# One transformer layer on one core: attention's weight folds with gate blocks between them, the merge kept in SBUF, and longer loads in the planner's model

## The chip, the core and the metric

The kernel runs on one core of a Trainium2 chip. The metric is the device time of one execution in microseconds, lower is better. A figure for the kernel is the median of several runs.

## What is computed

One layer for 1024 frames of width 1024, all in float32. A normed input h is projected to the inputs of two recurrent branches and to two merge gates; the branches' outputs are merged, and cross attention to 256 memory tokens and an MLP follow.

```python
h = rmsnorm(x, norm_mix_g)
proj = h @ w_in                      # ..., gate_a, gate_b
y_a = o_a @ w_branch_gdn             # gated DeltaNet branch
y_b = o_b @ w_branch_gla             # gated linear attention branch
merged = sigmoid(gate_a) * y_a + sigmoid(gate_b) * y_b
x = x + merged @ w_out
q = rmsnorm(x) @ wq;  k = rmsnorm(mem) @ wk;  v = rmsnorm(mem) @ wv     # 4 heads
x = x + softmax(q k^T / 16) v @ wo
x = x + relu(rmsnorm(x) @ w1)**2 @ w2
out = rmsnorm(x)
```

## The kernel before, in words

**Precision and engines.** A product in float32 is made of three matmuls in a reduced float format (`mm3`, L529): the high part of both factors, high times low, low times high (L534, L536, L538). `split` (L572) makes the two parts of an operand: ACT copies the high part (L574), DVE or POOL subtracts it for the low part (L575). Weights come by DMA from the SP queue into a tile `raw` (L503, four buffers), are split into `wop` and `wlo` tiles, and are used by PE (TensorE). A result leaves PSUM by an operation of ACT or DVE (VectorE); there are four PSUM buffers named `pd` and four named `ps`.

**Stages.** In order of the program: phase 0 (norms, and all of cross attention that depends on memory alone), four gate blocks, the linear attention branch (GLA), the DeltaNet branch, the merge, the output projection, attention, the MLP. Most large products use a seven-product scheme for 2x2 blocks (`wino`, p = 0..6).

**Phase 0** (`phase0`, L678). `project("wk", u)` and `project("wv", u)` make keys and values of the memory tokens, a quarter (u) at a time, from two 512 KB loads each: K0..K3, V0..V3, 48 matmuls of 256 columns each. Their results go to tile `kv` (L724, L725), which has one buffer, for keys first, for values later. `fold_q(h)` multiplies the query weights of a head with its keys, so that attention needs no queries (Q0..Q3, 48 matmuls of 256 columns each); DVE evicts to `gst` (L740, three buffers), and a DMA from the ACT queue stores it to `Gd`. `fold_o(h)` does the same for the output weights and values (O0..O3, 24 matmuls of 512 columns each); ACT evicts (L754), stored to `Ud`. The order is K0..K3, Q0..Q3, V0, O0, V1, O1, V2, O2, V3, O3. Between them `x_norm` norms each half of x: sums, a reciprocal root, eight scalings by DVE (L764) and eight splits into `hb`, which the gates and GLA read. `XO` names the blocks after which x is loaded, summed and normed.

**Gate blocks.** `push_gate` (L1438) multiplies h with 128 columns of the gate weights (48 matmuls of 512 columns), ACT takes tanh, and the result is stored to `tgd` in DRAM. Gates 0 to 3 run after phase 0; under them `t_sums` (L798) makes the sums of x that GLA's products need and splits them.

**The merge** (`phase_merge`, L1761). `yb` forms y_b for output blocks in two pairs; `yb_done` multiplies by the gate, read back from `tgd` through a ring of eight pieces in tile `A0b`, and stores the product to `m1d` in DRAM. `ya` forms y_a; `ya_done` reads gate and m1d back (two ring pieces for each block and half), multiplies and adds; the first four blocks go to `md` in DRAM and are read back by `staged` (L1549), the last four are split at once. `put` splits the merged blocks into `B0a`/`B0b` and `B1a`/`B1b`, which the output projection reads.

**What sets the order.** A planner (`Plan`, L159) first records the whole program, then lists it again: `latest` works backwards from PE's times to a due time for each operation, `forward` simulates the engines and takes the ready operation that is due first, PE in program order among those that are ready. The result is a fixed order on each engine's queue; a waiting instruction holds all those behind it. Costs are in `Op` (L74): a DMA takes its bytes at 390 bytes per ns on one ring and 2050 ns to land.

Of the kernel before, what the change touches and what calls it, by code (L numbers as in the profile page):

```python
# [18 lines left out]
P = 128  # L19
# [22 lines left out]
XO = (('K3', 'Q1', 'V0'), ('V0', 'V1', 'O2'))  # L42
# [21 lines left out]
ROUNDS, TOP, PAD, WINDOW, LOAD, HORIZON = 4, 228656, 128, 3413, 1283, 30000  # L64
# [9 lines left out]
class Op:  # L74
# [6 lines left out]
    def __init__(self, ins, flex):  # L81
# [33 lines left out]
        if ins.opcode == "DMACopy":  # L115
            self.dma, self.cost, self.own, self.lat = True, 60, 2050, 2050
            self.bytes = n * 4 * outs[0].ap[0][1]
        elif eng == "tensor":
            m = size(ins_[0])
            if ins.is_transpose:  # L120
                self.cost = m * 0.85
            elif ins_[0].dtype == F32R:
                self.cost = m * 0.4463 + (4 if m < HALF else 0)
            elif m == 64:
# [34 lines left out]
class Plan:  # L159
# [119 lines left out]
    def latest(self, deps, at, end):  # L279

        ops, n = self.ops, len(self.ops)
        last = [end] * n
        users, order = [0] * n, []
        for d in deps:
            for j in d:
                users[j] += 1
        todo = [i for i in range(n) if not users[i]]
        while todo:
            i = todo.pop()
            o = ops[i]  # L290
            s = last[i] = at[i] if o.eng == "tensor" else last[i] - o.cost
            for j in deps[i]:
                q = ops[j]
                if q.eng != "tensor":
                    last[j] = min(last[j], s - q.to(o, j in self.raw[i]) - q.bytes / 390)
                users[j] -= 1
                if not users[j]:
                    todo.append(j)
        return last

    def forward(self, deps, prio):
# [35 lines left out]
        def run(i, t):  # L337
# [18 lines left out]
            if o.dma:  # L356
                e = free["ring"] = max(e, free["ring"]) + o.bytes / 390
# [113 lines left out]
class Layer:  # L471
# [206 lines left out]
    def phase0(self, xp):  # L678
        nc, a = self.nc, self.a
        with ExitStack() as ctx:  # L680
# [1080 lines left out]
    def phase_merge(self, sp, ob):  # L1761
# [27 lines left out]

        def yb_done(u):  # L1790
            def done(i, half, x):
                nc.vector.scalar_tensor_tensor(x, get(), 1.0, x, ADD, MUL)
                self.nc.sync.dma_start(self.m1d[2 * u + i][:, hs(half)], x)
                more()
            return done
# [8 lines left out]
        x[0] = self.slot("A0a", (NB, HALF), F32)  # L1804
        srcs = []
        for us in pairs:
            for i, half in stages:
                for u in us:
                    srcs += [self.tgd[2 * u + i][:, hs(half)], self.m1d[2 * u + i][:, hs(half)]]
        get, more = fetcher(srcs)  # L1810
        for k in range(0, NB, 2):
            self.load(x[0][:, k:k + 2], a["xT"][:, k:k + 2, 0:HALF])
# [7 lines left out]
        def ya_done(u, last):  # L1820
            def done(i, half, c):
                ta, m1 = get(), get()
                nc.vector.scalar_tensor_tensor(c, ta, 1.0, c, ADD, MUL)
                nc.vector.tensor_tensor(c, m1, c, ADD)
                more()
                more()
                blk = 2 * u + i
                if not last:
                    nc.sync.dma_start(self.md[blk][:, half], c)
                elif half in mT:  # L1830
                    put(blk, half, c)
                else:
                    held.append((blk, half, c))
            return done

        def after(p):

            for half in range(2):
                if p == 2 * half + 1:
# [3 lines left out]
                    for blk in range(4):  # L1843
                        put(blk, half, self.staged(sp, self.md[blk][:, half]))
# [7 lines left out]
        x[1] = self.slot("A0b", (NB, HALF), F32)  # L1852
        for k in range(0, NB, 2):
            self.load(x[1][:, k:k + 2], a["xT"][:, k:k + 2, HALF:T])
# [365 lines left out]
    def run(self):  # L2220
# [7 lines left out]
        self.md = [dt([P, 2, HALF], f"md{b}") for b in range(4)]  # L2228
# [8 lines left out]
        self.m1d = [dt([P, T], f"m1d{k}") for k in range(NB)]  # L2237
# [5 lines left out]
        with ExitStack() as ctx:  # L2243
            self.wp = self.pool(ctx, "w1", "right")
            with ExitStack() as xctx:
# [3 lines left out]
                with ExitStack() as gctx:  # L2249
                    gp = self.pool(gctx, "gp", "right")  # L2250
                    for i in range(4):
# [3 lines left out]
                    self.until("g2")  # L2255
# [23 lines left out]
        with ExitStack():  # L2279
            self.phase_merge(sp, ob)  # L2280
            self.phase_out(sp)
            self.phase_attn(sp)
# [102 lines left out]
```

## Time and profile before

| | |
|---|---|
| median of 3 runs | 2214.92 us (2212.59 to 2218.59) |
| profiled execution | 2218.4 us |
| its span | 2216.6 us |
| mean granted clock | 0.991 |
| PE busy | 2160.5 us, 97% |
| DVE busy | 1702.1 us, 77% |
| ACT busy | 1092.8 us, 49% |
| moved by DMA | 300.20 MB |

Times inside the profile count from the start of the span. A row of windows gives, for a stretch, the busy time of each engine with the number of its instructions (x), the share of TensorE's full clock that was granted, the busy share of the 16 DMA engines and what they moved in GB/s. A row of waits names the engine and tile that waited, the one that ended the wait, and total, number and longest. A row of groups gives busy time and the mean in ns of one, then the idle time before them.

### The profile page before, as it was taken

What the parts mean: (1) busy time and instruction counts of PE and PEld (TensorE: products, weight loads), DVE (VectorE), ACT (ScalarE), POOL (GpSimd) and SP (SyncE); (2) the same over time, 40 slices, a digit from 0 to 9 for tenths busy, and PEclk for the clock granted to TensorE, in tenths of its full rate; (3) what the DMA queues carried; (4) which work ended last, traced back from release to release, by engine and by line L of the source; (5) the groups of instructions that cost most, each with busy time, mean ns of one, the idle gap of its engine ahead of it and who ended that gap; (6) DMA issues with size and microseconds to landing.
All of it is one profiled execution on the core that took longest, in us unless ns stands there. A gap on an engine that the chain in (4) does not pass through costs nothing.

```text
span 2216.6 us, 32151 instructions
## 1 busy us (share of the span) xinstructions
PE 2160.5 (97%) x11504; PEld 1835.2 (83%) x11504; DVE 1702.1 (77%) x3161; ACT 1092.8 (49%) x2215; POOL 208.2 (9%) x242
## 2 busy tenths in 40 slices
PE   8899999999999999999999999999999999999996
PEld 8788878988889888888878778998788888887876
DVE  7776997778796978969689965479989777567666
ACT  5544555354455545555544343465655555433433
POOL 0000000010220323222110000000100000000001
PEclk9999999999999999999999999999999999999998
DMA  8842122121311112112177841255354445687752
GB/s 273 273 153 73 59 101 86 57 83 49 120 38 50 65 47 74 48 35 76 40 248 256 285 175 67 77 168 184 116 184 142 152 157 182 212 265 249 239 175 84
DMA packets 147311, 300.20 MB, mean 135 GB/s; under 512 B 15688, under 2 KB 22216, under 8 KB 147152
## 3 DMA queue, kind: packets, MB, share of 16 engines
q1 hardware_dynamic: 140352, 289.75, 39.5%
q10 hardware_dynamic: 6800, 8.42, 1.1%
q8 instruction: 90, 1.47, 0.3%
q14 instruction: 69, 0.57, 0.1%
HBM read 212.35 MB, written 85.75 MB: 134 GB/s over the span
## 4 chain that ended last, share of the span: by engine, by line
PE 71%; DMA 11%; DVE 11%; ACT 2%; issue 2%; SPq 1%; POOL 0%; DVEq 0%; ACTq 0%; POOLq 0%
PE pd L538 18%; PE pd L534 18%; PE pd L536 18%; DMA raw<-in_w_dram 3%; PE ps L534 2%; PE ps L538 2%; PE ps L536 2%; DVE wop L575 2%; PE ps L606 1%; DMA e<-ad 1%; PE ps L1327 1%; DMA Gd<-gst 1%; SPq L503 1%; DMA A0b<-tgd 1%; DMA rawa<-pd 1%
## 5 line engine op out<-in xcount | busy, mean ns | idle before, releaser
L574 ACT ACTIVATE wop<-raw 128x512 fp32r<-128x512 f32 (+1 forms) x472 | 312.6, 669 | 377.1 <-PE pd L538 174.6
L575 DVE TENSOR_TENSOR wop<-raw,wop 128x512 fp32r<-128x512 f32 (+1 forms) x435 | 309.6, 713 | 79.4 <-ACT wop L574 77.4
L1185 DVE SCALAR_TENSOR_TENSOR acc<-pd,convw,acc 128x511 f32<-128x511 f32 x144 | 106.8, 742 | 15.7 <-ACT acc L1182 15.5
L538 PE MATMUL pd<-t,wop 128*128 128x512 f32 x268 | 107.9, 402 | 0.1
L534 PE MATMUL pd<-t,wop 128*128 128x512 f32 x268 | 106.0, 395 | 1.3 <-ACT wop L574 1.3
L536 PE MATMUL pd<-t,wop 128*128 128x512 f32 x268 | 105.1, 392 | 0.0
L534 PE MATMUL pd<-B1a,wop 128*128 128x512 f32 (+1 forms) x220 | 82.9, 377 | 0.3 <-ACT wop L574 0.3
L538 PE MATMUL pd<-B1a,wop 128*128 128x512 f32 (+1 forms) x220 | 82.8, 376 | 0.1
L538 PE MATMUL pd<-A1a,wop 128*128 128x512 f32 x180 | 73.5, 409 | 2.3 <-DVE wop L575 2.3
L534 PE MATMUL pd<-A1a,wop 128*128 128x512 f32 x180 | 72.4, 402 | 2.7 <-DVE u L1723 2.0
L536 PE MATMUL pd<-A1a,wop 128*128 128x512 f32 x180 | 71.7, 399 | 0.0
L574 ACT ACTIVATE whi<-raw 128x512 fp32r<-128x512 f32 x70 | 42.0, 626 | 55.3 <-PE pd L536 50.1
L536 PE MATMUL pd<-B0b,wop 128*128 128x512 f32 x172 | 67.6, 393 | 0.9 <-DVE B0b L575 0.9
L534 PE MATMUL pd<-A1b,wop 128*128 128x512 f32 x144 | 57.8, 402 | 3.3 <-DVE u L1723 3.3
L534 PEld LDWEIGHTS pd<-t,wop 128*128 128x128 f32 x268 | 50.4, 188 | 12.7 <-ACT wop L574 2.0
L538 PEld LDWEIGHTS pd<-t,wop 128*128 128x128 f32 x268 | 50.4, 188 | 12.6 <-DVE wop L575 1.0
L536 PEld LDWEIGHTS pd<-t,wop 128*128 128x128 f32 x268 | 50.4, 188 | 11.6
L538 PE MATMUL pd<-A1b,wop 128*128 128x512 f32 x144 | 57.5, 399 | 0.1
L536 PE MATMUL pd<-B1a,wop 128*128 128x512 f32 (+1 forms) x156 | 57.3, 367 | 0.0
L536 PE MATMUL pd<-A1b,wop 128*128 128x512 f32 x144 | 56.9, 395 | 0.0
L534 PE MATMUL pd<-A0a,whi 128*128 128x512 f32 x140 | 55.6, 397 | 0.8 <-ACT whi L574 0.8
L538 PE MATMUL pd<-A1a,wlo 128*128 128x512 f32 x140 | 56.3, 402 | 0.0
(603 smaller groups left out, 6996.4 us busy)
## 6 DMA issues: line engine op xcount, KB each, us to landing
raw<-in_w_dram SPq DMA_DIRECT2D x120, 256.0 KB, 3.9
raw<-in_w_gdn_dram SPq DMA_DIRECT2D x64, 256.0 KB, 2.8
raw<-in_w_dram SPq DMA_DIRECT2D x32, 512.0 KB, 4.4
e<-ad SPq DMA_DIRECT2D x63, 256.0 KB, 4.7
ad<-q SPq DMA_DIRECT2D x45, 256.0 KB, 2.6
rawa<-ad SPq DMA_DIRECT2D x42, 256.0 KB, 4.6
A0b<-tgd SPq DMA_DIRECT2D x32, 256.0 KB, 4.9
ad<-acc SPq DMA_DIRECT2D x30, 256.0 KB, 2.3
```

Source lines behind the costliest of these rows:

```text
L503: self.nc.sync.dma_start(dst, src)
L534: nc.tensor.matmul(out, lh, rh, start=first and i == 0, stop=False)
L536: nc.tensor.matmul(out, lh, rl, start=False, stop=False)
L538: nc.tensor.matmul(out, ll, rh, start=False, stop=last and i == n - 1)
L574: nc.scalar.activation(hi, raw, AF.Copy)
L575: (lo_eng or nc.gpsimd).tensor_tensor(lo, raw, hi.bitcast(F32), SUB)
L606: self.nc.tensor.transpose(pt[:, i * P:(i + 1) * P], s, self.ident)
L1185: nc.vector.scalar_tensor_tensor(x, pt[:, 0:HALF - d], tap, x, MUL, ADD)
L1327: nc.tensor.matmul(pt[0:96, i * n:(i + 1) * n], PF[:, v + i, 0:96], Z, start=True, stop=True)
```

## The change

1. Phase 0 makes all keys and values first; `kv` gets two buffers. Then the folds follow with gates 0 to 2 between them: Q0, Q1, g0, Q2, O0, g1, Q3, O1, g2, O2, O3. The new `gate` takes tanh into a tile with the tag `mraw`. Only gate 3 runs after phase 0. `XO` moves the norms of x accordingly.
2. The merge keeps its eight blocks in SBUF, four in slot `A0a` and four in a new pool `m`. The tensors `m1d` and `md` go; the ring holds gates alone. The first half of x is loaded to `A0a` only after its blocks are split.
3. The planner's model: a DMA lands after 2600 ns instead of 2050 and moves 300 bytes per ns instead of 390; an ACT instruction with a broken access pattern costs 140 ns more, a second output of one that reads SBUF 240 instead of 385; a small matmul is recognised by either side.

```diff
-XO = (('K3', 'Q1', 'V0'), ('V0', 'V1', 'O2'))
+ORDER = ('Q0', 'Q1', 'g0', 'Q2', 'O0', 'g1', 'Q3', 'O1', 'g2', 'O2', 'O3')
+XO = (('K3','V1','V3'),('V1','V3','Q1'))
...
-            self.dma, self.cost, self.own, self.lat = True, 60, 2050, 2050
+            self.dma, self.cost, self.own, self.lat = True, 60, LAND, LAND
...
-            self.cost, self.own, self.lat = d - 100 + (240 if psum(ins_[0]) else 385) * (len(outs) > 1), 130, 135
+            self.cost, self.own, self.lat = d - 100 + 240 * (len(outs) > 1) + 140 * broken, 130, 135
...
-                e = free["ring"] = max(e, free["ring"]) + o.bytes / 390
+                e = free["ring"] = max(e, free["ring"]) + o.bytes / RATE
...
-                    kv[which] = self.til(sp, [P, 2, NB, MEM], "kv", F32R, bufs=1)
+                    kv[which] = self.til(sp, [P, 2, NB, MEM], "kv", F32R, bufs=2)
...
-            for u in range(4):
-                self.push(f"K{u}", project("wk", u))
-            for h in range(XH):
-                self.push(f"Q{h}", fold_q(h))
-            for u in range(4):
-                self.push(f"V{u}", project("wv", u))
-                self.push(f"O{u}", fold_o(u))
+            tanh = {}
+            def gate(i):
+                def evict(half, pt):
+                    if i // 2 not in tanh:
+                        tanh[i // 2] = self.til(sp, [P, NB, MEM], "mraw", bufs=1).rearrange("p a b -> p (a b)")
+                    o = (2 * (i % 2) + half) * HALF
+                    t = tanh[i // 2][:, o:o + HALF]
+                    nc.scalar.activation(t, pt, AF.Tanh, scale=0.5)
+                    nc.sync.dma_start(self.tgd[i][:, half * HALF:(half + 1) * HALF], t)
+                return self.g_fm(lambda: self.wpart(a["w_gate"][i], [NB, P], nc.vector, sp), evict)
+            for which, x in (("K", "wk"), ("V", "wv")):
+                for u in range(4):
+                    self.push(f"{which}{u}", project(x, u))
+            makes = {"Q": fold_q, "O": fold_o, "g": gate}
+            for x in ORDER:
+                self.push(x, makes[x[0]](int(x[1])))
...
+        m = [self.slot("A0a", (4, T), F32), self.til(self.mp, [P, 4, T], "m")]
+        mb = lambda blk, half: m[blk // 4][:, blk % 4, hs(half)]
...
-                nc.vector.scalar_tensor_tensor(x, get(), 1.0, x, ADD, MUL)
-                self.nc.sync.dma_start(self.m1d[2 * u + i][:, hs(half)], x)
+                nc.vector.scalar_tensor_tensor(mb(2 * u + i, half), get(), 1.0, x, ADD, MUL)
...
-                ta, m1 = get(), get()
-                nc.vector.scalar_tensor_tensor(c, ta, 1.0, c, ADD, MUL)
-                nc.vector.tensor_tensor(c, m1, c, ADD)
+                blk = 2 * u + i
+                nc.vector.scalar_tensor_tensor(c, get(), 1.0, c, ADD, MUL)
                 more()
-                more()
-                blk = 2 * u + i
-                if not last:
-                    nc.sync.dma_start(self.md[blk][:, half], c)
-                elif half in mT:
+                to = c if last else mb(blk, half)
+                nc.vector.tensor_tensor(to, mb(blk, half), c, ADD)
+                if last and half in mT:
                     put(blk, half, c)
...
-                        put(blk, half, self.staged(sp, self.md[blk][:, half]))
+                        put(blk, half, mb(blk, half))
+                    if half:
+                        load_x(0)
...
-                    for i in range(4):
+                    for i in range(3, 4):
                         self.push_gate(i, lambda src: self.wpart(src, [NB, P], self.nc.vector), gp, "tg", 4)
```

The change moves instructions on every engine. Three places show it. The changed kernel's lines stand a little lower in its file (L505 there is L503 here, L1451 is L1436).

PE in phase 0, before: the last matmuls of V0 (they write `pd_901` and read the normed memory `mT`), then O0, which reads `kv`, the tile that V0's eviction fills.

```order
L538 MATMUL pd_901<-mT_206,wlo_896 128x256
L534 MATMUL pd_901<-mT_206,wop_895 128x256
L536 MATMUL pd_901<-mT_206,wop_895 128x256
L538 MATMUL pd_901<-mT_206,wlo_896 128x256
L534 MATMUL pd_966<-wop_955,kv_887 128x512
L536 MATMUL pd_966<-wlo_956,kv_887 128x512
L534 MATMUL pd_991<-wop_955,kv_887 128x512
```

PE in phase 0, now: the last matmuls of V3, then Q0, which reads `kv_195`, the keys' tile.

```order
L536 MATMUL pd_767<-mT_194,wop_761 128x256
L538 MATMUL pd_767<-mT_194,wop_761 128x256
L540 MATMUL pd_767<-mT_194,wlo_762 128x256
L536 MATMUL pd_832<-kv_195,wop_821 128x256
L538 MATMUL pd_832<-kv_195,wop_821 128x256
L540 MATMUL pd_832<-kv_195,wlo_822 128x256
```

The fold behind a projection no longer reads what that projection has just made.

The SP queue in the merge, before: ring loads for `ya` (gates `tgd` and products `m1d`, into `A0b`) with stores of finished blocks to `md` among them.

```order
L503 DMA A0b_12277<-tgd_101 128x512
L503 DMA A0b_12277<-tgd_100 128x512
L503 DMA A0b_12277<-m1d_160 128x512
L503 DMA A0b_12277<-m1d_161 128x512
L1829 DMA md_66<-acc_12481 128x512
L503 DMA A0b_12277<-tgd_102 128x512
L503 DMA A0b_12277<-m1d_162 128x512
L503 DMA A0b_12277<-tgd_103 128x512
L1829 DMA md_65<-q_12383 128x512
```

The SP queue there, now: gates alone, with weights of the DeltaNet branch's projection between them.

```order
L505 DMA A0b_12249<-tgd_97 128x512
L505 DMA A0b_12249<-tgd_96 128x512
L505 DMA A0b_12249<-tgd_98 128x512
L505 DMA A0b_12249<-tgd_96 128x512
L505 DMA A0b_12249<-tgd_99 128x512
L505 DMA A0b_12249<-tgd_98 128x512
L505 DMA A0b_12249<-tgd_97 128x512
L505 DMA raw_12471<-in_w_bgdn_dram 128x1024
L505 DMA A0b_12249<-tgd_99 128x512
```

All eight pieces of the ring are gates now, and no store stands between the loads.

The SP queue ahead of the merge, before: staged pieces of the linear attention's output (`obd`), stores of DeltaNet's (`oad`), then the first weights `w_bgla`.

```order
L503 DMA e_11364<-obd_71 128x512
L1436 DMA oad_78<-v_10733 128x512
L503 DMA e_11368<-obd_71 128x512
L1436 DMA oad_82<-v_10733 128x512
L503 DMA raw_11317<-in_w_bgla_dram 128x1024
L503 DMA raw_11318<-in_w_bgla_dram 128x1024
```

The same place now.

```order
L505 DMA e_11339<-obd_66 128x512
L1451 DMA oad_78<-v_10717 128x512
L505 DMA e_11343<-obd_67 128x512
L1460 DMA tgd_110<-acc_11440 128x512
L505 DMA raw_11301<-in_w_bgla_dram 128x1024
L505 DMA raw_11302<-in_w_bgla_dram 128x1024
```

Before, three of the four pieces of operand 2 (`obd_71`) are loaded ahead of the weights; now one of them (`obd_67`, the same operand) is.

More of the change, by code (lines that the diff above doesn't have):

```diff
@@ L123, in __init__ @@
                 self.cost = m * 0.4463 + (4 if m < HALF else 0)
-            elif m == 64:
+            elif max(m, size(ins_[1])) == 64:
                 self.cost = 80
@@ L294, in latest @@
                 if q.eng != "tensor":
-                    last[j] = min(last[j], s - q.to(o, j in self.raw[i]) - q.bytes / 390)
+                    last[j] = min(last[j], s - q.to(o, j in self.raw[i]) - q.bytes / RATE)
                 users[j] -= 1
@@ L1803, in phase_merge, with load_x @@
         x = self.xT = {}
[L1804 to L1812, printed above, removed]
+        get, more = fetcher([self.tgd[2 * u + i][:, hs(half)] for us in pairs for i, half in stages for u in us])
+        def load_x(half):
+            x[half] = self.slot(("A0a", "A0b")[half], (NB, HALF), F32)
+            for k in range(0, NB, 2):
+                self.load(x[half][:, k:k + 2], a["xT"][:, k:k + 2, hs(half)])
         def put(blk, half, c):
@@ L1851, in phase_merge @@
         self.drain()
-        x[1] = self.slot("A0b", (NB, HALF), F32)
-        for k in range(0, NB, 2):
-            self.load(x[1][:, k:k + 2], a["xT"][:, k:k + 2, HALF:T])
+        load_x(1)
     def sq_sum(self, sp):
```

16 lines of the change are left out of this document (8 added, 8 removed).

## The prediction

> **What bounds the kernel now.** I read the page first, then the windows by stage, then who waited for whom.
>
> ```profile
> PE 2160.5 (97%) x11504; PEld 1835.2 (83%) x11504; DVE 1702.1 (77%) x3161; ACT 1092.8 (49%) x2215; POOL 208.2 (9%) x242
> PEclk9999999999999999999999999999999999999998
> ```
>
> PE is the bound as a whole, but 97% hides waits, because the ends of matmuls are modelled. Counts in a window show them:
>
> ```profile
> core 0: us, PE busy (x) PEld busy (x) DVE busy (x) ACT busy (x) POOL busy (x), PEclk, DMA share, GB/s
> 28.00:42.00 14.00, 14.00 (x121) 14.00 (x120) 9.42 (x17) 5.51 (x8) 0.00 (x0) 1.00 0.73 220
> 1750.00:1800.00 50.00, 50.00 (x221) 41.11 (x220) 38.20 (x60) 26.76 (x43) 0.00 (x0) 1.00 0.42 145
> ...
> 42.00:65.00 23.00, 18.35 (x147) 17.46 (x146) 14.49 (x30) 6.36 (x6) 1.01 (x1) 1.00 0.88 282
> 65.00:125.00 60.00, 54.44 (x310) 46.82 (x309) 47.43 (x71) 39.31 (x62) 4.70 (x3) 0.94 0.74 243
> ...
> 1243.00:1298.00 55.00, 49.01 (x196) 36.45 (x195) 52.60 (x87) 19.71 (x34) 0.00 (x0) 0.96 0.82 291
> 1280.00:1303.00 23.00, 18.11 (x63) 12.98 (x62) 21.60 (x36) 9.84 (x17) 0.00 (x0) 0.85 0.51 173
> ```
>
> At full pace a matmul of 256 columns takes 14/121 = 0.116 us, one of 512 takes 50/221 = 0.226 us. So 42 to 65 us (Q folds) lost 23 - 147 x 0.116 = 5.9 us, and 1243 to 1298 us (end of the merge) lost 55 - 196 x 0.226 = 10.7 us. The granted clock fell in two places: 0.94 over 60 us is 3.6 us lost, 0.85 over 23 us is 3.4 us. Elsewhere nearly every window has its 221. The change aims at these two places, so the waits there are what can be won.
>
> **Keys' and values' projections first, gates between the folds.** Who waited up to 125 us: PE first, then DVE, then the stores of a fold's results (size and median landing).
>
> ```profile
> PE pd L534 <- ACT mT L689: 5.4, 1, 5.4
> PE pd L534 <- ACT kv L724: 5.4, 3, 3.3
> PE pd L534 <- DVE gst L740: 4.6, 4, 1.5
> ...
> DVE gst L740 <- DMA Gd<-gst: 12.4, 7, 3.1
> ...
> Gd<-gst ACTq DMA_DIRECT2D x16, 256.0 KB, 5.5
> ```
>
> - The wait for kv (5.4 us): each O fold stood right behind the projection whose result it reads, and waited for that eviction on ACT and DVE. Now V3 is followed by Q0, which reads keys of long ago, and O0 comes three blocks after V3. I take all 5.4 as gone.
> - The wait for gst (4.6 us): sixteen Q evictions in a row, three gst buffers, 5.5 us to land each: three evictions per 5.5 us plus the eviction, while PE makes one per 12 x 0.116 = 1.4 us. Four PSUM buffers absorb the first eight or so; the window before 42 us, with the first Q folds, is at full pace. Now at most two folds (eight evictions) stand together, then a gate gives 48 x 0.226 = 10.8 us to catch up. I take 4.0 of 4.6.
> - The clock (3.6 us): it fell after these waits, so it goes with them. In all 13.0 us.
> - What is late next: DVE. Its pieces are these.
>
> ```profile
> L575 DVE TENSOR_TENSOR wlo<-raw,wop 128x1024 fp32r<-128x1024 f32 (+1 forms) x34 | 39.4, 1158 | 7.9 <-PE pd L536 3.9 <-PE pd L538 2.0 <-ACT wop L574 1.6
> ...
> L740 DVE TENSOR_TENSOR gst<-pd,rmb 128x256 f32<-128x256 f32 x32 | 12.0, 418 | 12.4 <-DMA Gd<-gst 12.4
> L764 DVE SCALAR_TENSOR_TENSOR x<-x,cols,ps 128x512 f32<-128x512 f32 x16 | 11.8, 740 | 1.8 <-PE ps L631 1.8
> ...
> L575 DVE TENSOR_TENSOR A1a<-x,A1a 128x512 fp32r<-128x512 f32 x4 | 2.8, 688 | 0.0
> ```
>
> From Q0 to O0 (Q0, Q1, g0, Q2, O0) PE has 3 x 48 x 0.116 + (48 + 24) x 0.226 = 33 us. DVE has nine splits of weights (9 x 1.16), 24 evictions (24 x 0.418) and the second half of x (8 x 0.740 + 8 x 0.688): 31.9 us, without its waits for stores. The second half of g0 needs that half of x, so what DVE waits in Q0 and Q1 comes out on PE. The 12.4 us for sixteen evictions are 0.8 us for each; eight make 6 us. I take 4 us of new PE waits, with bounds of 0 (all hidden by the Q2 matmuls that the new order slips into g0) and 9 (0.8 for twelve evictions). Net: -13.0 + 4 = -9 us, bounds -13 and -4.
> - Gates: their 144 matmuls are the same work elsewhere; the tanh is the same ACT work; each gate's load of 0.5 MB and two stores of 256 KB move into the folds. What hides them: a pair of folds moves 8 x 256 KB out and 4 x 512 KB in, 4.2 MB, the gate behind it 1.05 MB; 5.2 MB in 22 us is 240 GB/s, below the 282 of the second row above. Cost 0, or 2 us if a pair's 4.2 MB in 11 us isn't prefetched.
> - t_sums and its splits lose three of four gates as cover (32.5 us of PE), but run in the folds and under g3 instead; DVE there has O2, O3 and g3, 21.7 us, with few evictions (O's are on ACT). Cost 0; without that cover some 5 us.
> - The second kv buffer adds no instruction.
>
> **Merge's blocks on chip.** Out go 16 stores and 16 loads of m1d, 8 stores and 8 loads of md. PE's waits from 1120 to 1310 us, DVE's and the SP queue's from 1196 to 1298 us:
>
> ```profile
> PE pd L534 <- ACT wop L574: 3.2, 2, 2.6
> PE pd L534 <- ACT B0a L574: 2.8, 1, 2.8
> PE pd L538 <- DVE wop L575: 1.2, 3, 0.5
> PE pd L536 <- DVE B0b L575: 0.9, 1, 0.9
> ...
> DVE raw L1634 <- DMA raw<-in_w_bgdn_dram: 2.6, 2, 1.5
> DVE acc L1823 <- DMA A0b<-tgd: 1.9, 1, 1.9
> DVE q L1681 <- DMA m1d<-q: 1.0, 1, 1.0
> ...
> SPq L1793 <- DVE q L1792: 7.2, 4, 4.5
> SPq L503 <- DMA A0b<-m1d: 5.5, 3, 4.9
> ```
>
> DVE was busy 52.6 of the last 55 us, and its arithmetic is unchanged: the same two operations for each block and half, the same splits. So the transfers are not the bound there; DVE's backlog is, and only the waits that let it build can go. The waits for tgd (the ring now holds eight gates ahead, not four pairs) and for the m1d store are 1.9 + 1.0 us; SP's 7.2 + 5.5 us of blocked queue no longer hold weight loads back, worth part of the 2.6. I take 3.3 us off the backlog, and one of the two half-clock stretches (1.7 us): -5 us. Bounds: 0 (DVE merely waits elsewhere) and -10.7 (all of the loss). x of the first half now loads after A0a is free; its adds run on DVE while four PSUM buffers cover 4 x 24 x 0.226 = 21.7 us of PE, so I cost it 0, or one 5 us landing.
>
> [...]
>
> **The plan's model of loads and of ACT.** It reorders SP, DVE and ACT everywhere, PE hardly after the folds. At the merge's start weights are now issued two staged loads earlier; of the 3.2 us above I take 1.5 (bounds 0 and 2.7). For the rest, the nearest rows are the two worst windows of the last projection, which has the same PE order:
>
> ```profile
> 2000.00:2050.00 50.00, 46.55 (x194) 36.66 (x193) 35.90 (x56) 19.47 (x35) 3.82 (x3) 0.97 0.79 253
> ...
> 2100.00:2150.00 50.00, 46.73 (x196) 37.30 (x195) 38.23 (x60) 21.45 (x37) 3.84 (x3) 0.97 0.64 197
> ```
>
> They lost 27 x 0.226 = 6.1 and 25 x 0.226 = 5.7 us. A model with slower loads could win half of that or double one: I take 0, bounds -6 and +6.
>
> **The sum.** -9 - 5 - 1.5 + 0 = -15.5 us. The profiled execution took 2218.4 us, which is 2202.9 after; its time is 3.5 above the median 2214.92, so on that median I forecast 2199.4.
>
> **Rivals.**
> 1. *DVE bounds the folds.* For: 31.9 us of work under 33 us of PE. Against: PSUM and the gates give slack. Then 9 us of new waits instead of 4: 2204.
> 2. *The merge stays DVE-bound.* For: 52.6 of 55 us busy, nothing taken off. Against: DVE did wait for tgd. Merge gives 0: 2204.
> 3. *All losses go.* Folds -13, merge -10.7, start -2.7: 2188.5. Against: DVE in both places.
> 4. *The rest eats it.* The reordered loads cost 6 us in the last projection and rival 1 and 2 hold in part: about 2210, no difference.
> 5. *Slower.* Loads that are issued earlier stand at the head of the one SP queue and wait there for their buffer, with every later load behind them; the last projection lives on that queue at 0.79 of the DMA engines. It decides from 15.5 us of new PE waits there, 1.3 times what the two windows lose now (11.8); at twice that, +23.6 - 15.5 gives 2223. Against: the PE order and the buffers there are unchanged.
>
> [...]
>
> **How the numbers follow.** Forecast 0.52, rivals 1 and 2 0.13 each, 3 0.06, 4 0.09, 5 0.07. 0.3% of 2214.9 is 6.6 us, about what can be told from no change, so faster means below 2208.3: forecast, rivals 1 to 3 nearly whole: 0.81; same 0.12; slower 0.07. The range takes in rivals 1 to 4 and most of the bounds: 2186 to 2211.
>
> **What would show it.** Right: up to the first GLA block PE waits for kv are gone, those for gst below 1 us, the clock there 1.00; the stretch before GLA about 9 us shorter; in the merge no transfers of m1d and md, DVE still near full, 196 matmuls in some 50 us. Wrong: PE waits in g0's second half of over 9 us; a merge as long as before; new waits in the last projection of more than 6 us.

## The result and the profile after

The changed kernel takes 2186.02 us (median of 4 runs, 2185.93 to 2186.22), the kernel before beside it 2215.36 us (4 runs, 2212.59 to 2218.59). The ratio is 0.9867, 95% interval 0.985 to 0.9884: 29.3 us faster, where 15.5 were forecast. The profiled execution took 2185.99 us, its span is 2183.9 us, its mean granted clock 0.996.

First the page of the changed kernel: busy time by engine, and the chain of work that ended last.

```profile
PE 2147.0 (98%) x11504; PEld 1832.2 (84%) x11504; DVE 1689.9 (77%) x3167; ACT 1097.7 (50%) x2215; POOL 198.0 (9%) x236
...
PE 85%; DVE 2%; DMA 1%; issue 0%; ACT 0%; DVEq 0%; ACTq 0%
```

PE makes the same 11504 matmuls. DVE is busy for 1690 us instead of 1702, and the transfers fall from 300.20 to 287.62 MB. What went on PE is waiting, and time at a lower clock: it is idle for 36.9 us of the span instead of 56.1, and the mean granted clock is 0.996 instead of 0.991. To see where, I cut the span at the first eviction of each stage. GLA's start is the first start in the row of ACT's `qk` evictions in a trace, here before, then after:

```profile
L888 ACT ACTIVATE qk<-pd x3: 579/580/584, 170.7 to 381.4; 128x512 f32<-128x512 f32 x3
```

```profile
L903 ACT ACTIVATE qk<-pd x3: 584/599/600, 168.0 to 378.3; 128x512 f32<-128x512 f32 x3
```

The other cuts are found in the same way (first eviction of `yb`, of the output projection, first relu). Single executions scatter, so both kernels were profiled a second time: in the rows marked "again", whose programs are the same on every engine.

| us by stage | phase 0 | GLA, DeltaNet | merge | output, attention | MLP |
|---|---|---|---|---|---|
| before | 170.7 | 960.6 | 169.1 | 288.4 | 627.9 |
| before, again | 168.0 | 962.6 | 168.2 | 290.5 | 621.4 |
| after | 168.0 | 957.2 | 157.7 | 285.5 | 615.5 |
| after, again | 167.0 | 957.0 | 158.0 | 285.5 | 615.6 |
| mean change | -1.9 | -4.5 | -10.8 | -4.0 | -9.1 |

The two profiles of before differ by up to 6.5 us in one stage, those of after by 1.0 at most. The 12.4 us by which the first pair of profiles differs in the MLP are 9.1 on the mean of two. The forecast put most of the gain in phase 0; it has the smallest part. Of the four signs that were to show phase 0 right, two are there, the waits that were to go; a granted clock of 1.00 and a stretch that is 9 us shorter are not. PE's waits to 125 us, after:

```profile
PE pd L536 <- ACT mT L691: 5.7, 1, 5.7
PE pd L540 <- DVE wlo L577: 3.0, 4, 1.5
PE ps L619 <- DVE acc L645: 2.0, 2, 1.5
PE pd L536 <- ACT wop L576: 0.6, 1, 0.6
```

The waits for `kv` (5.4 us) and for DVE's `gst` (4.6 us) are gone. New ones are for DVE's low parts of weights (`wlo`) and for the sums of squares (`acc`). The windows say where, after:

```profile
core 0: us, PE busy (x) PEld busy (x) DVE busy (x) ACT busy (x) POOL busy (x), PEclk, DMA share, GB/s
15.00:30.00 15.00, 13.20 (x101) 13.01 (x101) 12.32 (x25) 9.89 (x17) 3.02 (x2) 0.93 1.04 394
30.00:45.00 15.00, 13.89 (x110) 13.52 (x110) 12.26 (x19) 10.25 (x18) 1.13 (x1) 0.96 0.39 124
45.00:60.00 15.00, 12.77 (x103) 12.14 (x102) 15.00 (x21) 10.06 (x16) 3.81 (x4) 1.00 0.44 138
```

A full 15 us holds 15 / 0.116 = 129 products of 256 columns. The three windows have 314 where 387 would fit: some 73 x 0.116 = 8.5 us lost in the projections of keys and values, with DMA at a busy share of 1.04 in the first and DVE busy for all of the third. Now the merge, after: its last 55 us, and DVE's longest waits from 1120 to 1290 us.

```profile
1228.00:1283.00 55.00, 55.00 (x242) 45.10 (x241) 54.49 (x92) 20.92 (x36) 0.00 (x0) 1.00 0.40 128
```

```profile
DVE wop L577 <- ACT wop L576: 5.2, 4, 1.8
DVE q L1838 <- DMA A0b<-tgd: 1.6, 1, 1.6
```

242 products in 55 us are full pace (243), not the 196 of before, and DVE is still busy for 54.49 of the 55 us. In the last projection the two bad windows, after, are full as well (the work in them lies some 20 us further on, since the MLP starts that much earlier), and so are the other windows from 1850 to 2150 us:

```profile
2000.00:2050.00 50.00, 50.00 (x221) 41.04 (x220) 38.08 (x61) 21.43 (x36) 2.56 (x2) 1.00 0.77 248
2100.00:2150.00 50.00, 50.00 (x224) 41.35 (x223) 27.09 (x43) 14.48 (x23) 1.68 (x1) 1.00 0.22 64
```

In the second profile of before the first of these windows is as bad as in the first profile, the second nearly full:

```profile
2000.00:2050.00 50.00, 47.19 (x199) 37.62 (x198) 36.20 (x57) 19.59 (x35) 3.77 (x3) 0.97 0.79 249
2100.00:2150.00 50.00, 49.77 (x218) 40.40 (x217) 35.94 (x57) 21.61 (x37) 3.99 (x3) 1.00 0.65 198
```

They lose 22 and 3 products, 5.7 us. So of the 11.8 us that I had read there, some 6 came with that one execution.

### The profile page after: what moved, and what is told of

It is laid out like the page before. It is cut to its first block, busy times and chain, and to the rows that moved or that the text cites. A ratio compares the mean times of both kernels' runs of the same rounds, so it can differ in the third digit from the quotient of the medians.

```text
span 2183.9 us, 32078 instructions
## 1 busy us (share of the span) xinstructions
PE 2147.0 (98%) x11504; PEld 1832.2 (84%) x11504; DVE 1689.9 (77%) x3167; ACT 1097.7 (50%) x2215; POOL 198.0 (9%) x236
## 2 busy tenths in 40 slices
DMA packets 140399, 287.62 MB, mean 132 GB/s; under 512 B 14920, under 2 KB 21448, under 8 KB 140240
## 4 chain that ended last, share of the span: by engine, by line
PE 85%; DVE 2%; DMA 1%; issue 0%; ACT 0%; DVEq 0%; ACTq 0%
PE pd L540 19%; PE pd L536 19%; PE pd L538 19%; PE ps L536 5%; PE ps L540 5%; PE ps L538 5%; PE ps L608 2%; PE ps L1342 1%; PE ps L1333 1%; PE ps L1382 1%; PE ps L1399 1%; PE ps L1262 1%; PE ps L1276 1%; PE ps L1074 1%; PE ps L1389 1%; PE ps L1373 1%
## 5 line engine op out<-in xcount | busy, mean ns | idle before, releaser
L577 DVE TENSOR_TENSOR wop<-raw,wop 128x512 fp32r<-128x512 f32 (+1 forms) x429 | 303.4, 709 | 97.1 <-ACT wop L576 94.1
L1200 DVE SCALAR_TENSOR_TENSOR acc<-pd,convw,acc 128x511 f32<-128x511 f32 (+1 forms) x144 | 106.0, 740 | 13.2 <-ACT acc L1197 13.1
L536 PE MATMUL pd<-A1a,wop 128*128 128x512 f32 x180 | 71.2, 396 | 2.3 <-DVE ex L896 2.3
L538 PE MATMUL pd<-A1a,wop 128*128 128x512 f32 x180 | 70.8, 393 | 0.3 <-DVE A1a L577 0.3
L540 PE MATMUL pd<-A1a,wop 128*128 128x512 f32 x168 | 67.6, 402 | 0.0
L577 DVE TENSOR_TENSOR wlo<-raw,wop 128x1024 fp32r<-128x1024 f32 (+1 forms) x37 | 44.9, 1218 | 24.9 <-PE pd L540 15.3
L540 PE MATMUL pd<-A0b,wlo 128*128 128x512 f32 x152 | 61.1, 402 | 0.0
L540 PE MATMUL pd<-A1a,wlo 128*128 128x512 f32 x152 | 60.7, 399 | 0.0
L540 PE MATMUL pd<-A0a,wlo 128*128 128x512 f32 x152 | 60.3, 397 | 0.1
L540 PEld LDWEIGHTS pd<-t,wop 128*128 128x128 f32 x268 | 50.4, 188 | 11.7
L536 PEld LDWEIGHTS pd<-t,wop 128*128 128x128 f32 x268 | 50.4, 188 | 10.9
L540 PE MATMUL pd<-A1b,wlo 128*128 128x512 f32 x152 | 59.5, 392 | 0.0
```

What stands on the lines that cost most here:

```text
L536: nc.tensor.matmul(out, lh, rh, start=first and i == 0, stop=False)
L538: nc.tensor.matmul(out, lh, rl, start=False, stop=False)
L540: nc.tensor.matmul(out, ll, rh, start=False, stop=last and i == n - 1)
L577: (lo_eng or nc.gpsimd).tensor_tensor(lo, raw, hi.bitcast(F32), SUB)
L1200: nc.vector.scalar_tensor_tensor(x, pt[:, 0:HALF - d], tap, x, MUL, ADD)
```

## The experiments

Theory M: the new model of the planner, costed at 0 in the forecast, brought most of the gain, because loads are issued in time for ACT and DVE. Rival T: the merge's removed transfers and the freed SP queue brought it. In all tables "ACT for loads" is the sum of ACT's waits for DMA from 1750 to 2150 us, the stretch that holds the staged loads of the last projection (the parts of its operand that are read back from `ad` in DRAM and split), "PE there" the sum of PE's waits in the same stretch.

### Each part alone, and all but the model

The three numbered parts of the change, each put alone into the kernel before, then the changed kernel with the old model.

```diff
+ROUNDS, TOP, PAD, WINDOW, LOAD, HORIZON, LAND, RATE = 4, 228656, 128, 3413, 1283, 30000, 2600, 300
...
+            self.cost, self.own, self.lat = d - 100 + 240 * (len(outs) > 1) + 140 * broken, 130, 135
...
```

> The kernel before with the new planner's model alone (2600 ns, 300 bytes per ns, the ACT costs); phase 0 and the merge as before. Theory M, the model brought what I had costed at 0: -5 us ahead of the merge, some -4 in the merge (transfers of m1d and md still there), -3 behind it and -12 in the last projection, about -22 us, 2193. Rival T, the transfers that the merge no longer makes, and the SP queue that they leave free, brought it: within 5 us of before, and the windows of the last projection from 2000 us on lose their 11.8 us as before.

```diff
-                self.nc.sync.dma_start(self.m1d[2 * u + i][:, hs(half)], x)
+                nc.vector.scalar_tensor_tensor(mb(2 * u + i, half), get(), 1.0, x, ADD, MUL)
```

> The kernel before with its merge on chip alone; phase 0 and the model as before. Theory M: the merge gives what the prediction took for it, 5 us, and at most 7; the last projection loses its 11.8 us as before; about 2209. Rival T: the merge's 11.4 us and the 15 us behind it come back here, some -25 us, about 2190.

```diff
+ORDER = ('Q0', 'Q1', 'g0', 'Q2', 'O0', 'g1', 'Q3', 'O1', 'g2', 'O2', 'O3')
+XO = (('K3','V1','V3'),('V1','V3','Q1'))
...
+                    kv[which] = self.til(sp, [P, 2, NB, MEM], "kv", F32R, bufs=2)
```

> The kernel before with its new phase 0 alone (keys and values first, gates 0 to 2 among the folds). In the trace of the changed kernel the start of GLA came 2.7 us earlier and GLA gave 1.9 of it back, so both theories expect -1 to -3 us here, 2212 to 2214. If the new order of the folds is worth the 9 us of the prediction and the new model took 6 of it away, it is 2206.

```diff
-            self.dma, self.cost, self.own, self.lat = True, 60, LAND, LAND
+            self.dma, self.cost, self.own, self.lat = True, 60, 2050, 2050
...
-            self.cost, self.own, self.lat = d - 100 + 240 * (len(outs) > 1) + 140 * broken, 130, 135
+            self.cost, self.own, self.lat = d - 100 + (240 if psum(ins_[0]) else 385) * (len(outs) > 1), 130, 135
...
-                e = free["ring"] = max(e, free["ring"]) + o.bytes / RATE
+                e = free["ring"] = max(e, free["ring"]) + o.bytes / 390
```

> The changed kernel with the old planner's model (2050 ns, 390 bytes per ns, the old ACT costs). Theory M: it loses the 5 us ahead of the merge, some 5 in the merge and the 15 behind it again: about 2208. Rival T: it keeps them, 2186 to 2190.

| | median us | ratio to before (95%) | phase 0 | merge | MLP | ACT for loads | PE there |
|---|---|---|---|---|---|---|---|
| model alone | 2188.28 | 0.9882 (0.9865 to 0.9899) | 166.4 | 162.7 | 616.9 | 50.4 | 0 |
| merge alone | 2208.16 | 0.9967 (0.9956 to 0.9978) | 168.6 | 163.7 | 625.6 | 120.9 | 5.5 |
| phase 0 alone | 2234.24 | 1.0085 (1.0063 to 1.0108) | 163.7 | 168.0 | 645.7 | 162.9 | 15.4 |
| changed, old model | 2231.37 | 1.0076 (1.0053 to 1.0099) | 164.5 | 162.6 | 651.4 | 166.3 | 18.0 |

Theory M holds in the main and rival T falls: the model alone gives 26.8 us of the 29.3. The merge alone gives 6.9 us, 4.5 to 5.4 of them in its stage, as the forecast had it. The parts do not add: alone they come to -26.8 - 6.9 + 19.1 = -14.6 us.

Phase 0 alone missed both theories, and so did the changed kernel with the old model: 2231.37 us, where theory M had 2208. Phase 0 alone does start GLA at 163.7 us, 4 to 7 us earlier than before, and is still 19 us slower, since the MLP, which it does not touch, takes 645.7 us. ACT's longest waits for staged loads in the last projection, in the changed kernel with the old model:

```profile
ACT t L575 <- DMA e<-ad: 18.7, 9, 4.8
ACT A1b L575 <- DMA e<-ad: 17.3, 6, 5.8
ACT B0a L575 <- DMA e<-ad: 15.8, 8, 5.1
```

The same in the changed kernel:

```profile
ACT B0a L576 <- DMA rawa<-ad: 7.6, 6, 2.3
ACT B0b L576 <- DMA e<-ad: 7.2, 7, 1.9
ACT A1b L576 <- DMA rawa<-ad: 6.0, 4, 3.3
```

The loads are the same in both (63 into `e`, 42 into `rawa`) and those into `e` land as fast, in 4.5 us at the median in both; with the old model ACT waits longer for them, 166.3 us in all instead of 58.4. What PE waited for there, changed kernel with the old model:

```profile
PE pd L535 <- DVE u L1737: 7.4, 3, 3.3
PE ps L535 <- ACT wop L575: 4.9, 10, 1.8
PE pd L535 <- DVE u L1695: 2.2, 1, 2.2
```

PE never waits for a load itself in this stretch; it waits for evictions (`u`, on DVE) and splits (`wop`, on ACT). ACT is the one that waits for the loads, and DVE there waits for ACT's splits of the operand, 18.1 us for those into `A1b` alone.

### Which half of the model

Now theory M1: it is the landing time and the rate of the loads, not ACT's costs (rival A), nor the luck of any new order (rival C).

```diff
-            self.cost, self.own, self.lat = d - 100 + 240 * (len(outs) > 1) + 140 * broken, 130, 135
+            self.cost, self.own, self.lat = d - 100 + (240 if psum(ins_[0]) else 385) * (len(outs) > 1), 130, 135
```

> The changed kernel with the old ACT costs (and the old rule for small matmuls) in the model, the new landing and rate of loads kept. Theory M1, it is the loads: the plan issues them early enough to land before ACT and DVE want them, so this stays within 4 us of the changed kernel, 2184 to 2190. Rival A, it is the ACT costs: about 2231, as with the whole old model. Rival C, any new set of costs gives another order and its luck: neither of the two, somewhere between 2190 and 2225.

```diff
-            self.dma, self.cost, self.own, self.lat = True, 60, LAND, LAND
+            self.dma, self.cost, self.own, self.lat = True, 60, 2050, 2050
...
-                e = free["ring"] = max(e, free["ring"]) + o.bytes / RATE
+                e = free["ring"] = max(e, free["ring"]) + o.bytes / 390
```

> The changed kernel with the old landing (2050 ns) and rate (390 bytes per ns), the new ACT costs kept. Theory M1: the losses of the old model in the last projection return, ACT's waits for staged loads there come to some 100 us again instead of some 30, and it takes 2220 to 2235. Rival A: it stays at 2186 to 2190. Rival C: between the two.

The kernel before with parts 2 and 3 of the change, its phase 0 as before (the edit is shown against the changed kernel):

```diff
-ORDER = ('Q0', 'Q1', 'g0', 'Q2', 'O0', 'g1', 'Q3', 'O1', 'g2', 'O2', 'O3')
-XO = (('K3','V1','V3'),('V1','V3','Q1'))
+XO = (('K3', 'Q1', 'V0'), ('V0', 'V1', 'O2'))
...
```

> The kernel before with the new model and the merge on chip, its phase 0 as before. If the new order of the folds gains nothing under the new model (GLA began 1.6 us later in the changed kernel than with the new model alone, the DeltaNet branch 2.3 us later), this is the fastest: 2188.3 less the 5 us by which the changed kernel's merge is shorter than that of the model alone, about 2183. If the new folds are worth something, it is 2187 or more.

```diff
-ROUNDS, TOP, PAD, WINDOW, LOAD, HORIZON, LAND, RATE = 4, 228656, 128, 3413, 1283, 30000, 2600, 300
+ROUNDS, TOP, PAD, WINDOW, LOAD, HORIZON, LAND, RATE = 4, 228656, 128, 3413, 1283, 30000, 3400, 250
```

> The changed kernel with still longer loads in the model: 3400 ns and 250 bytes per ns, so that 256 KB take 4.4 us, as the traces show (3.2 to 5.7 us from issue to landing), not 3.5 as in the change nor 2.7 as before. Theory M1: the waits that it removes are nearly gone already, so 2182 to 2190. Rival C: any time between 2185 and 2230.

In the next three the same line has 2600 and 390, 2050 and 300, 2500 and 310.

> The changed kernel with the new landing (2600 ns) and the old rate (390): 256 KB count as 3.3 us, where the change has 3.5 and the old loads 2.7. Theory M1 in its simple form, the lead in time is what counts: it is near the changed kernel, 2186 to 2193. If the rate counts for itself, since the ring then fills up in the plan and loads are spread, it is 2200 to 2206.

> The changed kernel with the old landing (2050 ns) and the new rate (300): 256 KB count as 2.9 us. Theory M1 by the lead alone: between the old loads' 2206 and the changed kernel's 2186, nearer the old, 2196 to 2204. If the rate counts for itself: 2186 to 2191.

> The changed kernel with 2500 ns and 310 bytes per ns, a small step back towards the old loads (256 KB count as 3.35 us instead of 3.5). Theory M1: nearly no difference, 2184 to 2190. Rival C, luck: as far off as any other, 2190 to 2225.

| changed kernel with | median us | ratio to before (95%) | phase 0 | merge | MLP | ACT for loads | PE there |
|---|---|---|---|---|---|---|---|
| old ACT costs | 2188.80 | 0.988 (0.985 to 0.9909) | 165.5 | 156.8 | 615.0 | 27.0 | 0 |
| old loads (2050, 390) | 2206.11 | 0.9952 (0.9938 to 0.9967) | 164.2 | 161.0 | 623.9 | 122.1 | 3.2 |
| old phase 0 | 2186.90 | 0.9867 (0.9844 to 0.989) | 168.2 | 158.8 | 616.0 | 40.8 | 0 |
| 3400, 250 | 2204.52 | 0.9945 (0.9926 to 0.9964) | 178.4 | 165.1 | 621.7 | 33.8 | 1.6 |
| 2600, 390 | 2196.52 | 0.9908 (0.9883 to 0.9933) | 164.5 | 155.8 | 622.0 | 104.2 | 2.9 |
| 2050, 300 | 2191.89 | 0.9881 (0.9863 to 0.9899) | 168.5 | 156.8 | 619.7 | 86.9 | 0.9 |
| 2500, 310 | 2185.39 | 0.9851 (0.9832 to 0.987) | 167.7 | 158.2 | 615.8 | 64.2 | 0.7 |

- With the new loads the old ACT costs lose 2.8 us, so rival A falls as the account of the whole. With the old loads the new ACT costs gain 25 us (2231.37 to 2206.11), which M1 had not expected; that time lies between the two, where rival C had it. With both halves old the MLP takes 651.4 us, with either one new 615.0 or 623.9, and there is little left for the other. A step of 100 ns and 10 bytes per ns changes nothing (2185.39): as far as one step shows, the gain of the new values is not the luck of one order. Under the old ones the MLP does swing with what stands ahead of it, from 621 to 651 us.
- M1's simple form, the longer the better, falls too. At 3400 and 250 the time is 18.5 us worse, 10.4 of it in phase 0. And landing and rate are not one sum: 2600 with 390 counts 3.3 us for 256 KB and lost 10.5 us (2196.52, between the two ranges expected), 2050 with 300 counts 2.9 and lost 5.9. In the columns the rate does two things: 300 instead of 390 costs the new phase 0 some 4 us (168.0 and 168.5 against 164.2 and 164.5), and it brings part of the gain behind it.
- The old phase 0 misses its 2183 and ties with the changed kernel, 2186.90: under the new model the new order of the folds brings nothing. Up to 170 us PE's waits for `kv` are 1.0 us in it instead of the 5.4 before, in the old order, and those for `gst` 7.9.

The old model counts 2.7 us for 256 KB (2050 ns, and the bytes at 390 per ns). The staged loads of the last projection, in a stretch where the DMA engines move 242 GB/s (1790 to 2080 us), take longer; here in the changed kernel, with the median from issue to landing at the end:

```profile
e<-ad SPq DMA_DIRECT2D x63, 256.0 KB, 4.5
```

### The last projection's own loads

The kernel before, with the new landing and rate for the loads recorded from the MLP on. PE's order is word for word that of before, the other engines' as far as the MLP.

```diff
+        self.plan.late = len(self.plan.trace())
         self.phase_mlp(sp)
...
         for i, ins in enumerate(self.trace()):
+            LOADS[:] = (2050, 390) if i < self.late else (2600, 300)
```

> The kernel before with the new landing and rate for the loads of the MLP alone (all that is recorded behind attention); old ACT costs, phase 0 and merge as before. Theory M1, the loads of the last projection come earlier by their own due times: ACT's waits for staged loads from 1750 to 2150 us fall from 126 to below 80 us, PE's 6.7 us there go, the span behind the first relu falls from 628 to 616 to 620 us and the time to 2203 to 2207. Rival C: it is the whole order, not these loads: 2211 or more.

Two more profiles, of before and of this kernel, with no edit:

> The kernel before, unchanged, for a second profile of it. In the run with late loads for the MLP alone, the stages ahead of the MLP, the same instructions in the same order on each engine, read 4.2 us more than in the first profile of before. If that is the scatter of single executions, this profile's stages differ from the first by several us too, and the stage behind the first relu stays near 628 us. If before is steady (within 1 us by stage, as the changed kernel was in its two profiles but for phase 0), the late loads cost those 4 us.

> The kernel with late loads for the MLP alone, unchanged, for a second profile. Stage behind the first relu 615 to 617 us as before if its gain is the order's; the stages ahead as in either profile of before if their 4 us are scatter.

| | median us | ratio to before (95%) | ahead of the MLP | MLP | ACT for loads | PE there |
|---|---|---|---|---|---|---|
| before | 2215.36 | | 1588.8 | 627.9 | 125.8 | 6.7 |
| before, again | 2215.70 | 0.9996 (0.9979 to 1.0013) | 1589.2 | 621.4 | 115.7 | 2.9 |
| late loads | 2211.19 | 0.9975 (0.9964 to 0.9985) | 1592.9 | 615.5 | 75.5 | 0 |
| late loads, again | 2209.73 | 0.9972 (0.9956 to 0.9987) | 1592.0 | 617.4 | 78.9 | 1.5 |

The last projection's gain is shown to come from what the plan counts for its own loads: the order of the products is unchanged, ACT's waits fall to what was expected, and the stage falls by 8.2 us on the means. The rows of ACT's longest waits for loads there, first the two of before, then the one of the kernel with late loads, and then the two bad windows in the latter:

```profile
ACT A1a L574 <- DMA e<-ad: 18.1, 7, 6.7
ACT B0a L574 <- DMA e<-ad: 17.3, 7, 6.1
```

```profile
ACT t L576 <- DMA e<-ad: 9.1, 6, 2.8
```

```profile
2000.00:2050.00 50.00, 50.00 (x221) 41.27 (x220) 38.03 (x60) 20.73 (x36) 4.18 (x3) 1.00 0.82 266
2100.00:2150.00 50.00, 50.00 (x220) 41.02 (x219) 35.41 (x56) 22.01 (x37) 5.49 (x4) 1.00 0.64 194
```

The time fell by only 5.5 and 6.1 us against the runs of before beside each, short of the 8 to 12 expected, and the first time, 2211.19, is by itself in rival C's range. The profiles show why: both have some 3.5 us more ahead of the MLP (on the means) with the same order there. It came in both, so scatter alone is no likely cause; what makes it is open.

What the two values change is an order, and not simply how early a load is issued. PE makes its products in the same order in the last projection of all these kernels, so one can count how many it has made when a staged load is issued. With phase 0 alone the 105 loads are issued 79 products earlier than in before (median), and ACT waits longer, 162.9 us; at 3400 and 250 they are issued only 5 products earlier, and ACT waits 33.8 us. What broadly goes with the waits is the other work that ACT does between a load's issue and its split: on the mean 1.8 us in before, 1.9 in the changed kernel with the old model, 2.1 with late loads, 2.9 in the changed kernel and 3.0 at 3400 and 250. This is read from the traces; no run changed that distance alone. What the model gains ahead of the MLP was not followed to single waits.

Over all 19 profiles the waits of ACT and of PE go together: where ACT waited up to 87 us for loads from 1750 to 2150 us, PE waited 1.6 us at most in that stretch; with 104 to 126 us it was 2.9 to 6.7, with 163 to 166 us 10.6 to 18.0.

### Phase 0 under the two models

In the first kernel for this the two values were read only when the plan was made, so all loads had the new ones and the program was the changed kernel's, on every engine: it is "after, again" above, 2184.99 us, 0.9851 (0.9832 to 0.987).

> The changed kernel with the old landing and rate for what is recorded up to gate 3 (phase 0) and the new ones behind it. In the runs so far the new folds bring GLA's start to 163.7 to 164.5 us with the old loads, and to 165.5 to 168.0 with the new; behind that start the new loads take 2016 to 2022 us in all and the old 2037 to 2069. Theory S, the two are separate: 164.2 + 2016 = 2180 us of span, 2182 of time, and below the changed kernel's 2186 by some 4. Rival C, the order behind phase 0 is a matter of luck and changes with any change ahead of it: 2190 or more, and the stages behind GLA's start differ from the changed kernel's by more than 4 us.

The second one switches by the place of an instruction in the recorded program.

```diff
+                    self.plan.gla = len(self.plan.trace())
                     self.queue_gla()
...
         for i, ins in enumerate(self.trace()):
+            LOADS[:] = (2050, 390) if i < self.gla else (2600, 300)
```

> The changed kernel with the old landing and rate for the instructions recorded up to gate 3 and the new ones for all behind. (The run before that was meant for this read the two numbers only when the plan was made, so that all loads had the new ones: it was the changed kernel once more.) Theory R: with 300 bytes per ns the plan sees PE waiting for weights in the first 30 us and puts the sums of the memory and of x among the projections (after 52 and 128 products, where the old rate has them after 104 and 388), and DVE pays for x's norm there. With the old rate for phase 0 GLA starts at 164 to 165 us instead of 168, the rest stays as in the changed kernel, 2016 us: 2181 to 2183, the fastest of all. Rival C, the rest changes with what stands ahead of it: 2187 or more.

2182.01 us, ratio 0.9846 (0.9833 to 0.986), five runs from 2181.28 to 2184.77: the lowest median of the study. It is 4.0 us below the changed kernel's 2186.02, but only 3.0 below the 2184.99 of the same program above, whose four runs (2183.72 to 2187.83) overlap with these five and whose ratio hardly differs; the gain that is shown is the earlier start of GLA. GLA's start, and the three windows, in this kernel:

```profile
L905 ACT ACTIVATE qk<-pd x3: 582/600/600, 164.2 to 374.6; 128x512 f32<-128x512 f32 x3
```

```profile
15.00:30.00 15.00, 15.00 (x130) 15.00 (x129) 13.16 (x26) 13.53 (x26) 2.82 (x2) 1.00 0.98 350
30.00:45.00 15.00, 15.00 (x129) 15.00 (x129) 12.54 (x18) 10.32 (x17) 0.00 (x0) 1.00 0.75 259
45.00:60.00 15.00, 15.00 (x130) 15.00 (x129) 9.48 (x16) 6.78 (x10) 1.01 (x1) 1.00 0.63 191
```

Each window has its 129 products, and the granted clock is 1.00 where it was 0.93 and 0.96. Theory R's order is there: with the old values x's sums stand on PE after the projections (after 388 products), with the new ones among them (after some 128), and DVE's x norm with them: DVE is busy for 9.48 us of the last window instead of 15.00. That the plan does so because it believes PE would otherwise wait for weights is argued from its rules, not measured.

The last one takes the gates from between the folds, on phase 0 alone with the old model.

```diff
-ORDER = ('Q0', 'Q1', 'g0', 'Q2', 'O0', 'g1', 'Q3', 'O1', 'g2', 'O2', 'O3')
+ORDER = ('Q0', 'Q1', 'Q2', 'Q3', 'O0', 'O1', 'O2', 'O3', 'g0', 'g1', 'g2')
```

> The kernel before with the new phase 0, old model, as in the run of phase 0 alone, but the folds in a row: Q0 to Q3, O0 to O3, then gates 0 to 2. It is read by GLA's start, 163.7 us with the gates between. By the prediction's terms the waits for gst come back (4.0 us, and a part of the clock's 3.6): 167 to 171. Rival K, only moving V ahead of the folds counts (the waits for kv, and DVE's norm of x out of them): 163 to 165.

2251.88 us (2 runs), 1.0159 (1.0141 to 1.0178). GLA starts at 174.7 us, 11.0 later than with the gates between:

```profile
L902 ACT ACTIVATE qk<-pd x3: 579/579/586, 174.7 to 385.3; 128x512 f32<-128x512 f32 x3
```

That is more than the terms for `gst` and the clock, and later than before the change. PE's waits there up to 190 us:

```profile
PE pd L535 <- ACT gst L755: 5.2, 6, 2.5
PE ps L632 <- DVE rs_o L570: 2.9, 3, 1.5
PE pd L539 <- DVE wlo L576: 2.7, 5, 0.9
```

With the gates between they are 1.2, 0.6 and 0.3 us. The `gst` waits did come back, but at the O folds' evictions on ACT, not at those of the Q folds on DVE. Rival K falls: with the values' projections ahead and the gates at the end phase 0 loses 4 to 7 us, so the mixed order is what gains; gates between the folds and O folds among the Q folds were not tried apart.

## Why the prediction was wrong

- *The step that failed* is "A model with slower loads could win half of that or double one: I take 0", with 1.5 us at the merge's start. The model alone measured -26.8 us. By its stages against the means of before that is 3 in phase 0, 4 in GLA and DeltaNet, 6 in the merge, 7 behind it and 8 in the MLP. I had the rows for it: two windows of the last projection with 11.8 us of loss, DMA at 0.79 and DVE at 36 of 50 us busy, so that no engine was the bound and something had to be late (some 6 of the 11.8 us were that one execution's, by the second profile, but the stage gained 9.1 on the means). I did not ask ACT's waits what. They held 125.8 us for loads, 121.5 of them for staged ones, which landed far later than the 2.7 us that the plan counted. In before, from 1750 to 2150 us:

```profile
e<-ad SPq DMA_DIRECT2D x63, 256.0 KB, 4.7
```

- *Folds and phase 0, -9 us* (bounds -13 and -4): measured -1.9 on the means. With the old loads the new order gives 4 to 7 us, inside the bounds or at their edge, and the new waits come where I had put them, for x's norm in g0. In phase 0 alone:

```profile
PE pd L535 <- ACT A1b L575: 1.5, 1, 1.5
PE pd L537 <- DVE A0a L576: 0.9, 1, 0.9
PE ps L632 <- DVE rs_o L570: 0.6, 1, 0.6
```

What failed is the place of "4 us of new PE waits", from Q0 to O0, under the new rate: they came as 8.5 us of missing products in the projections ahead, because x's norm moved there. Where it is moved back, in the kernel with two models, GLA starts 2.7 to 3.7 us earlier. Each part was costed by itself, and these two act on each other.
- *Merge on chip, -5 us*: right for that part alone (4.5 to 5.4 in its stage). The argument behind its upper bound was wrong: "DVE's backlog is" the bound. The merge runs at full pace with DVE busy for 54.49 of 55 us. DVE has just enough time if it does not wait earlier: its waits from 1120 to 1290 us come to 9.6 us, 18.7 before. With the model alone, all transfers still there at 273 GB/s, the last 55 us of the merge (1232 to 1287) are as full, 242 products, and its stage is 5.9 us shorter. The two gains do not add in the time: on top of the model the merge on chip brings only 1.4 us (2188.28 to 2186.90; by the ratios to before, 0.9882 and 0.9867, some 3).
- *Rival 5*, new waits in the last projection, has the right place, and its cause does not show: the MLP lost 21 and 27 us against the mean of before with the old loads (phase 0 alone, and the changed kernel with the old model), where ACT waited longest for staged loads, and with the new ones that was gone. SP's own waits from 1800 to 2150 us hardly differ: 217 us in before, 224 with phase 0 alone, 207 in the changed kernel. Too long a model does lose, 18.5 us at 3400 and 250, most of it in phase 0; what does it there was not tried.
- *Rival 3*, all losses go (2188.5 us), is the case nearest the measurement, by other terms: its 13 us in the folds did not come, the MLP's did.
- *The clock*: I held that it fell after PE's waits and goes with them. In the projections after the change it fell to 0.93 and 0.96 from 15 to 45 us, where the longest wait is 1.5 us (the row for `acc` above), and it is 1.00 in the kernel with two models, where PE loses no product there. From 45 to 60 us after the change the longest wait is 1.5 us too (for `wlo`) and the clock stays at 1.00, so which waits bring it down is not shown. No run shows the term of 1.7 us, one of "two half-clock stretches" in the merge: the trace of before has a single one there, at 0.50 from 1294 to 1300.5 us, 3.3 us of loss, and after the change the merge's end is at 1.00 (its row above).

## What to carry to other kernels

A number in a planner's cost model is an edit of every stage: compare it with the landing times in the trace, and read who waits for loads on the helper engines, not only on the bound one. Where no engine is busy all the time and PE still loses products, look for waits on a helper's queue: from 2000 to 2050 us before, PE lost 27 products with DVE busy for 35.9 and ACT for 19.5 of the 50 us, and the plan's order alone won them back (221 products with late loads). The value nearest to the landing time in the trace need not be the best: 3400 and 250, 4.4 us for 256 KB, lost 18.5 us. Test parts that share a scheduler together, and profile a kernel twice before a single window of it is priced.

## What the hardware showed that I had not expected

The DMA engines moved 394 GB/s from 15 to 30 us at a busy share of 1.04 (the row of windows above). The highest rate in the rows of the prediction is 291. Staged loads of 256 KB took 4.5 us to land, at the median, with the engines moving 242 GB/s. And before scatters by several us from one execution to the next (2210.59 to 2222.82 in 15 runs). The changed kernel kept within 0.3 us in its first four, but the same program, taken again, spread over 4.1 us (2183.72 to 2187.83), so that steadiness is not shown.
